# Attention on one core: the sums of K blocks for later batches on Pool instead of VectorE

## The chip, the core and the metric

The kernel runs on one core of a Trainium2 chip. The core has engines with queues of their own: TensorE (PE, matrix products), VectorE (DVE), ScalarE (ACT), Pool or GpSimd (POOL) and SyncE (SP, which here only issues transfers). Each engine runs its queue in order; between engines, semaphores order the work. The metric is device time in microseconds (us) of one launch, the median of several runs; lower is better.

## The reference

Attention without a mask, 8 batches, 2048 rows of q, k and v each, 512 columns, float32 in and out:

```python
scores = np.matmul(q, k.transpose(0, 2, 1)) / np.sqrt(d_k)
attn_weights = special.softmax(scores, axis=-1).astype(np.float32)
return np.matmul(attn_weights, v)
```

## The kernel before

**Fewer products, more sums.** Both large products are cut into 2 x 2 blocks and made with seven block products instead of eight (the Strassen-Winograd scheme). It needs sums and differences of blocks of each operand. For the scores, S^T = K Q^T, the left operand is K transposed: with its blocks a11, a12, a21, a22 four more are formed, s1 = a21 + a22, a21 = a11 - a21 (in place), s2 = s1 - a11, s4 = a12 - s2. `k_sums` (L177 to L185) makes these four for one chunk of 4 x 128 rows of K; each is one two-input instruction over 128 partitions x 512 columns in float16, all in SBUF. A batch has four chunks, `c` = 0 to 3, each with its own tiles `kraw{c}`, `ks1_{c}`, `ks2_{c}`, `ks4_{c}`; every batch overwrites those of the batch before. Likewise `q_sums` (L194) makes the sums for Q, `v_sums` (L209) those for V, and `p_sums` (L325) those for the exponentials P.

**What comes from where.** A chunk of k or q is loaded and cast to float16 by a transfer on POOL's queue (`load`, L109, into one of three `stage` buffers), and transposed by a transfer on SP's queue (`dma_transpose`, L140, into `kraw` or `qraw`). V is loaded on POOL's queue (`load_v`, L204). Results leave through SP's queue (`store`, L400).

**The main loop** (L672 to L695) runs over 32 groups `g`, four to a batch (`qt` = 0 to 3), in 28 slots each. In a slot TensorE has one of the seven products for the scores of a block that is one half batch ahead (`Group.product`, L262: 2 matmuls of 512 columns, weights from `kraw` or `ks`) and, in every second slot, one of the seven products P V (`Pair.product`, L355: 8 matmuls of 256 columns). The order of all this is written out by hand (`ORDER`, L451; `QORDER`, L456), and each engine's queue follows the program's order.

What follows a score product: a copy of x by ACT (L298), copies into `cz` by ACT (L303, L306), two additions by VectorE out of PSUM (L309 after product 7, L312 after product 3), and exponentials by ACT (L227). What follows P V: a reciprocal (L413, L419) and scaling additions (L396) on VectorE, scaled copies (L393) on ACT, and a store. The sums of P stand in slots 7 to 13 (second pair), 17 to 22 and 4 to 5 (first pair of the next group); those of Q in slots 23 to 27 of odd groups and 6 of even ones; those of V in slots 0 to 20 of a batch's first group.

**The work around the change.** `prefetch` (L483) places the next batch's loads, transposes and K sums into slots. `PLAN` (L465) says where loads and transposes stand; `KSUMS` (L480) says in which slot the four sums of a chunk are put into the queue `background`; one is taken out in each of the slots 2, 8, 10, 14, 16, 24 and 26:

```python
(0, 10, "load", "k", 0), (0, 20, "trans", "k", 0),
(0, 22, "load", "k", 1), (1, 7, "trans", "k", 1),
(1, 8, "load", "k", 2), (1, 20, "trans", "k", 2),
(1, 22, "load", "k", 3), (2, 7, "trans", "k", 3),
KSUMS = {(1, 8): 0, (1, 20): 1, (2, 6): 2, (2, 20): 3}
```

The pairs are (qt, slot). The first products that use the new chunk 0 stand in the group with qt = 2, slot 0; chunk 1's in slot 14; chunks 2 and 3 follow in qt = 3, slots 0 and 14. The first batch's own K sums are made before and in group 0, from other calls of `k_sums` (L638, L641, L533).

POOL's queue holds, in the main loop, the 84 loads for batches 1 to 7 and one small fill of a constant.

Of the kernel before, what the change touches and what calls it, by code (L numbers as in the profile page):

```python
# [12 lines left out]
def kernel(  # L13
# [21 lines left out]
    nc = tc.nc  # L35
# [73 lines left out]
    def load(what, b, c, pieces=(CH,), room=None):  # L109
        t = staged.get((what, b, c))  # L110
        if room is not None:
            t = staged[what, b, c] = room
        if t is None:
            t = staged[what, b, c] = stage.tile([P, CH, D], F16, tag="stage", name="stage")
        n = CH - sum(pieces)
        for w in pieces:
            at = c * CH + n
            nc.gpsimd.dma_start(out=t[:, n:n + w, :], in_=srcs[what][b, :, at:at + w, :])
            n += w
# [20 lines left out]
    def dma_transpose(what, b, c):  # L140
        src = staged.pop((what, b, c))
        dst = raw_of(what, b, c)
        nc.sync.dma_start_transpose(
            out=dst[:, 0:CH].rearrange("p n c r -> p (n c) r"),
            in_=src[:].rearrange("p n d -> p (n d)"),
        )
# [20 lines left out]
    def k_blocks(c):  # L167
        w = kops[c][0][:].rearrange("p (j s) c r -> p j s c r", s=2)
        return w[:, :, 0, 0:2], w[:, :, 0, 2:4], w[:, :, 1, 0:2], w[:, :, 1, 2:4]
# [4 lines left out]

    add, sub = nc.vector.tensor_add, nc.vector.tensor_sub

    def k_sums(c):  # L177
        a11, a12, a21, a22 = k_blocks(c)
        _, s1, s2, s4 = kops[c]
        return [  # L180
            lambda: add(s1[:], a21, a22),
            lambda: sub(a21, a11, a21),
            lambda: sub(s2[:], s1[:], a11),
            lambda: sub(s4[:], a12, s2[:]),
        ]  # L185
# [18 lines left out]
    def load_v(b, c):  # L204
        dst = vraw[b % 2][:].rearrange("p j s d -> p (j s) d")
        ns = slice(c * CH, (c + 1) * CH)
        nc.gpsimd.dma_start(out=dst[:, ns, 0:D], in_=srcs["v"][b, :, ns, :])
# [272 lines left out]
    KSUMS = {(1, 8): 0, (1, 20): 1, (2, 6): 2, (2, 20): 3}  # L480
    background = deque()

    def prefetch(g, slot):  # L483
        b, qt = divmod(g, NQT)
        if (g, slot) == (0, 12):
            nc.gpsimd.memset(vraw[1][:, :, 1, D:D + 1], 1.0)
        for kind, what, c in PLAN.get((qt, slot), ()):
            if b + 1 < B:
                if kind == "load":
                    load_v(b + 1, c) if what == "v" else load(what, b + 1, c)  # L490
                else:
                    dma_transpose(what, b + 1, c)
        if (qt, slot) in KSUMS and b + 1 < B:
            background.extend(k_sums(KSUMS[qt, slot]))
        if background and slot in ((2, 8, 10, 14, 16, 24, 26)):
            background.popleft()()

# [130 lines left out]
    for n, (kb, half) in enumerate([(kb, 0) for kb in range(4, 8)] + [(kb, 1) for kb in range(8)]):  # L628
        if (kb, half) == (5, 0):
            pe_transpose("k", 1, 2, 4)  # L630
        if (kb, half) == (6, 0):
            pe_transpose("q", 1)
            background.extend(q_sums(0))
        if (kb, half) == (3, 1):
            pe_transpose("k", 2)
        if (kb, half) == (6, 1):
            pe_transpose("k", 3)
            background.extend(k_sums(3))  # L638
        plain_tile(kb, half, "qz" if n % 3 == 2 else "qx")
        if (kb, half) in ((3, 1), (7, 1)):  # L640
            background.extend(k_sums(kb // CH))  # L641
        step(2)
# [29 lines left out]
    for g in range(NP):  # L672
        todo = after_slot(g)
        sp = g // 2 + 1
        more = sp < NP // 2
        for slot in range(NS + 4):
            n, at = divmod(slot, len(QORDER))
            old, what = QORDER[at]
            if slot < NS:
                if more and at == 0:  # L680
                    cur = Group(sp, g % 2 * NG + n)
                if more and old == 0:
                    cur.product(what)
                if old == 1 and prev is not None:
                    prev.product(what)
                if at == 2 and prev is not None:
                    prev.exp_right()
                if at == len(QORDER) - 1:
                    prev = cur if more else None
                for f in sums_of(g, slot):  # L690
                    f()
            if slot in todo:
                pv(g, todo[slot])
            if slot < NS:
                prefetch(g, slot)  # L695
# [30 lines left out]
```

## Time and profile before

| | |
|---|---|
| time, median of 3 runs | 804.24 us (803.97 to 804.41) |
| span of the profiled execution | 801.4 us |
| busy: PE, DVE, ACT, POOL | 794.3, 557.6, 571.7, 72.3 us |
| K sums on VectorE (L181 to L184), whole run | 128 of 0.41 us each |
| sums of 128 x 1024 columns of P on VectorE (L338 to L341) | 192 of 0.68 us each |
| additions out of PSUM on VectorE (L309, L312) | 244 of 0.69 us each |
| issue of one load on POOL | 0.74 to 0.75 us |
| issue to landing, median: load of k, of q, of v | 7.0, 8.0, 10.7 us |
| issue to landing, median: transpose of k, of q | 7.1, 6.2 us |
| granted clock of TensorE | 1.00 |

The span runs from the first to the last instruction of the profiled execution; the runs' own times, of which the table gives the median, contain a little more than that. A line of an engine's timeline reads: start, duration, engine, line of the source, operation, tiles out<-in, shape, count, and in brackets the engine's idle time before it and what ended it. A matmul's duration in such a line is longer than the distance to the next one's start, since matmuls overlap in the array. "PEld" is the loading of a matmul's weights, which runs beside the matmul before it.

### The profile page before, as it was taken

How to read it: one execution, taken by the hardware profiler on the slowest of the kernel's cores; microseconds unless marked ns; L12 is line 12 of the kernel's file. 1: busy time of each engine (PE TensorE's matmuls, PEld its weight loads, DVE VectorE, ACT ScalarE, POOL GpSimd, SP SyncE). 2: the span in 40 equal slices, each digit the busy share in tenths (PEclk: the TensorE clock that was granted, in tenths of full speed). 3: DMA queues.
4: the chain of work that ended last, by engine and by line, in shares of the span. 5: the costliest groups of instructions: out<-in, count | busy, mean ns of one | idle time of the engine just before them, and what ended most of it. 6: DMA issues, size and time to landing. Idle time of an engine off the chain costs nothing.

```text
span 801.4 us, 14572 instructions
## 1 busy us (share of the span) xinstructions
PE 794.3 (99%) x5532; PEld 535.8 (67%) x5532; DVE 557.6 (70%) x1227; ACT 571.7 (71%) x1021; POOL 72.3 (9%) x105
## 2 busy tenths in 40 slices
PE   8999999999999999999999999999999999999998
PEld 5566666666666666666666666666666666666676
DVE  4786767857577675767758677586776857668464
ACT  5677777777767767777777777777677677776752
POOL 4011110011001011011000110001100011000000
PEclk9999999999999999999999999999999999999999
DMA  9999993999929999399974999749994598711112
GB/s 223 173 173 192 195 167 78 150 192 198 156 56 166 166 157 195 78 155 194 199 125 93 164 167 191 124 93 189 168 189 113 97 219 149 156 40 40 53 44 102
DMA packets 188150, 115.80 MB, mean 144 GB/s; under 512 B 122416, under 2 KB 170800, under 8 KB 188080
## 3 DMA queue, kind: packets, MB, share of 16 engines
q0 software_dynamic: 49648, 49.29, 42.8%
q1 hardware_dynamic: 138144, 65.29, 38.0%
q8 instruction: 43, 0.70, 0.4%
q10 hardware_dynamic: 288, 0.30, 0.1%
q14 instruction: 27, 0.22, 0.1%
HBM read 100.70 MB, written 33.55 MB: 168 GB/s over the span
## 4 chain that ended last, share of the span: by engine, by line
PE 98%; DMA 1%; ACT 1%; DVE 0%; SPq 0%; issue 0%
PE t L384 49%; PE t L287 46%; PE t L234 2%; PE tr L153 1%; DMA first<-in_k_dram 1%; PE t L247 0%; ACT right L227 0%; ACT o L393 0%; SPq L128 0%; DVE cz L309 0%; ACT stage L132 0%; ACT kraw L156 0%; ACT left L227 0%; ACT cz L306 0%; DVE qraw L156 0%
## 5 line engine op out<-in xcount | busy, mean ns | idle before, releaser
L287 PE MATMUL t<-qraw,kraw 128*128 128x512 f16 x728 | 197.1, 379 | 0.2 <-ACT left L227 0.2
L393 ACT ACTIVATE o<-t,r 128x256 f32<-128x256 f32 x256 | 121.6, 475 | 99.4 <-DVE r L413 67.5
L384 PEld LDWEIGHTS <-s 128*128 128x128 f16 x1536 | 150.2, 98 | 57.0
L227 ACT ACTIVATE left<-t 128x512 f16<-128x512 f32 (+1 forms) x260 | 154.7, 597 | 38.9 <-PE t L287 33.7
L396 DVE SCALAR_TENSOR_TENSOR o<-t,r,o 128x256 f32<-128x256 f32 x192 | 92.5, 482 | 105.0 <-PE t L384 48.7
L287 PEld LDWEIGHTS <-kraw 128*128 128x128 f16 x976 | 95.4, 98 | 64.1 <-issue 0.5
L287 PE MATMUL t<-qs,ks 128*128 128x512 f16 x488 | 135.3, 379 | 0.0
L384 PE MATMUL t<-vh,left 128*128 128x256 f16 x1024 | 133.0, 273 | 0.0
L384 PE MATMUL t<-vt,s 128*128 128x257 f16 (+1 forms) x1024 | 133.0, 273 | 0.0
L227 ACT ACTIVATE right<-cz 128x1024 f16<-128x1024 f32 x122 | 129.5, 1062 | 1.8 <-DVE cz L309 1.7
L384 PEld LDWEIGHTS <-right 128*128 128x128 f16 x1024 | 100.1, 98 | 38.3 <-issue 0.4
L384 PEld LDWEIGHTS <-left 128*128 128x128 f16 x1024 | 100.2, 98 | 37.6
L303 ACT COPY cz<-t 128x512 f32<-128x512 f32 x120 | 70.4, 587 | 72.7 <-PE t L287 72.3
L309 DVE TENSOR_TENSOR cz<-t,cz 128x512 f32<-128x512 f32 x122 | 83.8, 687 | 51.7 <-PE t L287 51.6
L312 DVE TENSOR_TENSOR cz<-t,cz 128x512 f32<-128x512 f32 x122 | 84.2, 690 | 38.5 <-PE t L287 38.2
L287 PEld LDWEIGHTS <-ks 128*128 128x128 f16 x732 | 71.5, 98 | 47.9
L287 PE MATMUL t<-qraw,ks 128*128 128x512 f16 x244 | 72.6, 379 | 0.0
L287 PE MATMUL t<-qs,kraw 128*128 128x512 f16 x244 | 72.6, 379 | 0.0
L298 ACT COPY t<-t 128x512 f32<-128x512 f32 x120 | 68.4, 570 | 4.1 <-PE t L287 1.0
L306 ACT COPY cz<-t 128x512 f32<-128x512 f32 x122 | 70.9, 582 | 0.0
L384 PE MATMUL t<-vt,right 128*128 128x256 f16 x512 | 67.1, 273 | 0.0
L384 PE MATMUL t<-vh,s 128*128 128x257 f16 x512 | 66.7, 273 | 0.0
(62 smaller groups left out, 576.5 us busy)
## 6 DMA issues: line engine op xcount, KB each, us to landing
out_dram<-o SPq DMA_DIRECT2D x127, 256.0 KB, 3.5
vh<-in_v_dram POOLq DMA_DIRECT2D x32, 512.0 KB, 10.7
stage<-in_q_dram POOLq DMA_DIRECT2D x28, 512.0 KB, 8.0
stage<-in_k_dram POOLq DMA_DIRECT2D x28, 512.0 KB, 7.0
right<-in_q_dram POOLq DMA_DIRECT2D x2, 512.0 KB, 9.8
right<-in_k_dram POOLq DMA_DIRECT2D x2, 512.0 KB, 11.7
first<-in_q_dram SPq DMA_DIRECT2D x2, 256.0 KB, 3.3
cz<-in_q_dram SPq DMA_DIRECT2D x2, 256.0 KB, 5.1
```

Source lines behind the costliest of these rows:

```text
L153: nc.tensor.transpose(tr[:, m, dc, :], src[:, n + m, dc * P:(dc + 1) * P], ident[:])
L227: nc.scalar.activation(out=out_, in_=in_, func=EXP, scale=inv_sqrt_d)
L234: nc.tensor.matmul(st[:], kops[c][0][:, n, dc, :], qraw[0][:, half * NT:(half + 1) * NT, dc, :], start=(dc == 0), stop=(dc == ND - 1),)
L287: nc.tensor.matmul(dst[:], lhs[:, j, dc, :], rhs[:, :, dc, :], start=(n in (1, 5) and dc == 0), stop=(dc == 1), skip_group_check=True,)
L298: f(out=self.y[:], in_=self.x[:])
L303: f(out=self.cz[:, 1, :], in_=self.z[:])
L306: nc.scalar.copy(out=self.cz[:, 0, :], in_=self.x[:])
L309: nc.vector.tensor_add(self.cz[:, 1, :], self.x[:], self.cz[:, 1, :])
L312: nc.vector.tensor_add(self.cz[:, 0, :], self.z[:], self.cz[:, 0, :])
L384: nc.tensor.matmul(dst[:, 0:width], lhs(j), rhs(j), start=(first and j == 0), stop=(j == NJ - 1), skip_group_check=True,)
L393: nc.scalar.activation(out=out_, in_=src, func=COPY, scale=r[:])
L396: nc.vector.scalar_tensor_tensor(out=out_, in0=src, scalar=r[:], in1=out_, op0=MULT, op1=ADD)
```

## The change

`k_sums` takes the engine as an argument, VectorE if none is given. The calls from `prefetch`, which make the sums for the second and later batches (7 batches x 4 chunks x 4 sums), give Pool; the first batch's keep VectorE. The places in the program stay the same, so these instructions move from VectorE's queue into POOL's, among the loads that `prefetch` issues there.

```diff
-    def k_sums(c):
+    def k_sums(c, engine=nc.vector):
         a11, a12, a21, a22 = k_blocks(c)
         _, s1, s2, s4 = kops[c]
+        add, sub = engine.tensor_add, engine.tensor_sub
         return [
             lambda: add(s1[:], a21, a22),
...
         if (qt, slot) in KSUMS and b + 1 < B:
-            background.extend(k_sums(KSUMS[qt, slot]))
+            background.extend(k_sums(KSUMS[qt, slot], nc.gpsimd))
         if background and slot in ((2, 8, 10, 14, 16, 24, 26)):
             background.popleft()()
```

In the built program, the queues of TensorE, ScalarE and SP hold the same instructions in the same order as before. VectorE's is shorter by 112 instructions. POOL's is longer by these 112 and by one that loads a library, ahead of the first of them. In a batch POOL's queue then reads: load k2; K0 s1, a21; load v1; K0 s2, s4; load k3; K1 s1, a21; load q2; K1 s2; load q3; K1 s4; load v2; K2 s1, a21, s2; load v3; K2 s4; K3 s1, a21, s2, s4; then the next batch's load q0.

## The prediction

> **What bounds the kernel now.** I read the shares of the page first, then the stretches, then the order of time on one engine after another around one batch's sums of K blocks.
>
> ```profile
> PE 794.3 (99%) x5532; PEld 535.8 (67%) x5532; DVE 557.6 (70%) x1227; ACT 571.7 (71%) x1021; POOL 72.3 (9%) x105
> PE 98%; DMA 1%; ACT 1%; DVE 0%; SPq 0%; issue 0%
> ```
>
> The second line is the chain that ended last: TensorE alone. The share of a busy PE is modelled, so I checked it against the spacing of starts, in the order of time on TensorE and in the table of stretches (span of the stretch, then busy time of PE, PEld, DVE, ACT, POOL):
>
> ```profile
> 180.38 1.04 PE L384 MATMUL t<-vh,s 128*128 128x257 f16 x8
> 181.26 0.59 PE L287 MATMUL t<-qs,ks 128*128 128x512 f16 x2
> 181.69 0.59 PE L287 MATMUL t<-qs,kraw 128*128 128x512 f16 x2
> 183.86 1.04 PE L384 MATMUL t<-vt,s 128*128 128x256 f16 x8
> 159.90:184.20 24.30, 24.30 (x171) 16.41 (x169) 15.84 (x34) 17.94 (x33) 5.09 (x7) 1.00 1.10 178
> 184.20:208.60 24.40, 24.40 (x171) 16.52 (x169) 17.68 (x40) 18.00 (x33) 1.48 (x2) 1.00 1.19 198
> ```
>
> A matmul of 512 columns starts every 0.215 us (0.59 less its own 0.38), one of 257 every 0.11 us, and no time is left over in the stretches, at a granted clock of 1.00. Idle of TensorE is 801.4 - 794.3 = 7.1 us, nearly all before the first batch's steady work and after the last scores. So VectorE, at 70%, has nothing to sell: unloading it can't shorten the chain. The change can only keep the time or lengthen it. A batch repeats every 97.46 us; I work with the one whose sums are wanted around 163 to 225 us.
>
> **The change, part by part.** *Removed from VectorE:* 7 batches x 4 chunks x 4 = 112 sums, 0.414 us each (the groups of L181 to L184, 0.412 to 0.416): 46.4 us, 6.6 us a batch. Worth nothing, since no matmul of the steady part waits for VectorE except one of 0.10 us a batch (154.7 us, waiting for the sums of V); 7 x 0.1 = 0.7 us is the most that relief could return, and that wait is over before the K sums begin. I count 0.
>
> *Added to POOL:* the same 112 sums, and one instruction that loads a library ahead of the first. POOL's queue holds its loads too, in program order: load k2, two sums of chunk 0, load v1, two sums, load k3, two of chunk 1, load q2, a sum, load q3, a sum, load v2, three of chunk 2, load v3, one, then chunk 3's four. POOL isn't tied to VectorE's place in the program, so a sum runs as soon as its transposed chunk has landed.
>
> *Is a sum late for TensorE?* Landings of chunks 0 to 3, from the tile view of kraw: 162.6, 177.5 (issued 168.52, the longest landing, 9.0), 181.0, 198.4. The first weight loads that want the sums come at 186.4, 198.5, 210.7 and 222.9, the last sum of a chunk some 2 us after. Between landing and need lie 23.8, 21.0, 29.7 and 24.5 us. Tightest is the whole run of chunks 1 to 3: twelve sums and four loads of 0.74 us between 177.5 and 224.9, (47.4 - 3.0) / 12 = 3.7 us a sum. Only a sum longer than that would be late. Nothing.
>
> *Loads behind the sums.* Load k3 starts at 163.19 now and goes behind four sums and load v1, 6 us later; it takes 7.0 us to land and its transpose is issued at 192.96: 16 us to spare. Load q2 (178.71) moves to about 181, wanted at 196.49, 8 us to land: 7 us to spare. v1 to v3 feed sums of the next batch, 40 us on. SP's queue keeps its order. Cost 0; without that cover each us of lateness would be one on TensorE.
>
> *The library.* No row shows it. Below: 0. Above: in the first batch chunk 0 lands at 70.7 and is wanted at 186.4 - 97.5 = 88.9, and POOL is free from 61.2 (load k2 at 60.44), so with four sums and a load still to come some 20 us is hidden. I take 0.
>
> *What a sum takes on POOL.* No two-input row on POOL exists. Lower end: 0.42 us, VectorE's. Upper end: POOL's memsets of 8 and 1 columns took 0.133 and 0.099 us, 4.9 ns a column; 512 of these and the 0.19 us of a one-column copy make 2.7 us. The geometric middle is 1.06; if POOL doesn't pair 16-bit elements, the lower end is VectorE's 32-bit 0.69 and the middle 1.36. I take 1.2.
>
> *What it does to VectorE.* This is where I expect the cost, and one pair of rows points at it:
>
> ```profile
> 38.79 0.69 DVE L198 TENSOR_TENSOR qs<-qraw 128x1024 f16<-128x1024 f16 x1 [1.01 <-DMA qraw<-right]
> 39.40 0.75 DVE L216 TENSOR_TENSOR vt<-vh,vt 128x512 f16<-128x512 f16 x2
> 38.83 0.70 POOL L620 CAST gate<-qraw 128x1 f32<-128x1 f16 x1 [22.97 <-DMA qraw<-right]
> 39.59 0.27 POOL L621 CAST gate<-vh 128x1 f32<-128x1 f16 x1
> ```
>
> A cast of one column on POOL took 0.70 us, and ended 0.05 us after the VectorE sum that had started before it; its twin ended 0.05 us after the first of the next two (39.40 + 0.41). The one without such company, L564, took 0.19. So POOL's read was held by a VectorE instruction with two SBUF inputs. The other direction no row shows: its bounds are no hold at all and a hold for a POOL sum's whole length. I take the whole length, since both casts were held to the very end. Instructions with one input in PSUM (L309, L312, L396) I take as free: L312 started beside POOL's load at 40.11 without growing.
>
> The Trainium skill says that it does: SBUF — State Buffer, section "Who interferes with whom", has an exclusive lock between a VectorE instruction with two SBUF inputs and a GpSimd one that reads SBUF; whoever starts first keeps it. No run here shows the direction that matters. By it the sum is the one below, without it zero. The GPSIMD Engine Reference, section "Performance versus the Vector engine", has 4497 ns for a two-input add of 2048 columns; a quarter is an estimate of 1.12 us, by which the walk below ends near 0.2 us a batch, at 805.6.
>
> **The walk** (VectorE's K sums taken out, 1.2 us a sum, 0.1 between dependent ones). VectorE and ScalarE now:
>
> ```profile
> 177.97 0.55 DVE L339 TENSOR_TENSOR s<-s,left 128x768 f16<-128x768 f16 x1
> 180.15 0.69 DVE L309 TENSOR_TENSOR cz<-t,cz 128x512 f32<-128x512 f32 x1 [1.09 <-PE t L287]
> 181.82 0.16 DVE L419 RECIPROCAL r<-t 128x1 f32<-128x1 f32 x1
> 182.23 0.68 DVE L199 TENSOR_TENSOR qs<-qraw,qs 128x1024 f16<-128x1024 f16 x1
> 188.81 0.28 DVE L338 TENSOR_TENSOR s<-right 128x256 f16<-128x256 f16 x1
> 182.02 0.47 ACT L393 ACTIVATE o<-t,r 128x256 f32<-128x256 f32 x1
> 182.86 0.61 ACT L227 ACTIVATE left<-t 128x512 f16<-128x512 f32 x1
> ```
>
> Chunk 0 (from 162.65): its four sums hold L338 or L339 by at most 1.2 us, with 0.9 to 1.4 us of idle time behind each. Chunk 1, first sum 177.55 to 178.75: L339 is held 0.78. Second sum 179.3 to 180.5: L340 is held, and behind it L309, wanted at 180.15, starts at 181.0, 0.85 late; the matmul that reuses its bank starts at 181.69, 0.85 after L309's end of 180.84: just covered. Load q2, third sum 181.24 to 182.44: L341 is held. Load q3, fourth sum 183.6 to 184.8. The reciprocal L419 comes 1.68 late, and with it ACT's L393, which ended at 182.49 and whose bank PE takes at 183.86: 1.37 of cover, so TensorE waits 0.28. ACT's L227 behind it (ended 183.47, bank taken at 184.73, 1.26) is 1.65 late: 0.39 in all. L199 is held to 184.8. Chunk 2 follows: its first sum holds L200, its third, 188.72 to 189.92, holds L338, which ends 1.1 late; the weight load that wants it comes 0.53 after its end, 0.92 with the wait already had: 0.2 more. Chunk 3 (198.4 on) meets sums with 1.5 to 2.5 us behind them: 0. A batch: 0.28 + 0.11 + 0.2 = 0.6 us; 7 batches 4.2 us.
>
> The profiled span is 801.4; the median of the runs lies 2.8 us above, which I take as outside the span and unchanged. 804.24 + 4.2 = **808.4 us**.
>
> **Rivals.** *No change:* VectorE isn't held, or a POOL sum is under about 1.1 us and every lateness stays inside 0.85, 1.37, 1.26 and 0.53. For: those covers; TensorE waits for nothing now. Against: the two casts. Time 804.2, at best 803.5 with the 0.7 us back. This is the side on which it isn't slower; the point is 0.85 us of lateness at L309.
>
> *A longer sum on POOL:* at 1.6 us the six waits before L338 grow by 0.4 each, 2.4 us, with the cover already spent: 3.0 a batch, 21 in all, 825 us. For: the memset slope (2.7 would give 9.6 a batch, 871). Against: a slope from eight columns is rough.
>
> *Late loads or sums:* needs 7 us of delay at q2 or 20 us of library. Each us beyond costs one: some 810, against it the spare times above.
>
> **How the numbers follow.** Forecast (805.9 to 815) 0.46; no change 0.30; longer sums (815 and up) 0.20; late loads 0.02; faster 0.02. About 0.2% (1.6 us) is what a measurement of this kernel tells from no change. Slower: 0.46 + 0.20 + 0.02 = 0.68; within 0.30; faster 0.02. The range holds the no-change case and most of the longer sums: 803.7 to 822; the forecast's own is 805.9 to 815.
>
> **What would show it.** After: 112 POOL sums of about 1.2 us in bursts after each landing; VectorE's two-input sums stretched beyond 0.68 only where such a burst runs, L309 and L312 not; gaps of 0.1 to 0.3 us on TensorE in the 15 us after chunk 1 has landed, none elsewhere. It is wrong if L339 keeps 0.68 us beside a POOL sum, if gaps come at the weight loads of ks, or if TensorE waits in stretches without POOL work.

## The result: 13 us slower, and the profile after

| | before | changed |
|---|---|---|
| time, median | 804.23 us | 817.11 us (813.21 to 820.93) |
| span of the profiled execution | 801.4 us | 819.1 us |
| ratio to before | | 1.0154, 95% interval 1.0130 to 1.0177 |

The forecast was 808.4 us: the direction and the mechanism came as forecast, the loss was 12.9 us instead of 4.2. The profiled execution of the changed kernel is the longest of its four (820.93 us). In the changed kernel every line from 178 on stands one further down: the first sum of Q, L198 before, is L199 now.

The busy shares and the chain that ended last, of the changed kernel:

```profile
PE 800.2 (98%) x5532; PEld 536.0 (65%) x5532; DVE 576.1 (70%) x1115; ACT 569.3 (70%) x1021; POOL 214.0 (26%) x217
PE 80%; DMA 8%; DVE 4%; POOL 3%; issue 2%; ACT 2%; SPq 0%; ACTq 0%; DVEq 0%; POOLq 0%
```

VectorE lost 112 instructions and is busy for 18.5 us longer than before. Its remaining two-input sums are longer than before by 56 us in all, counted by their lengths: an instruction that is held counts as busy. The chain, TensorE alone before, now runs through VectorE and POOL too, and through landings of transfers (8%, most of them those that release POOL's sums and those at the start). Groups of instructions (count, busy us, mean ns, idle time before):

```profile
L199 DVE TENSOR_TENSOR qs<-qraw 128x1024 f16<-128x1024 f16 x16 | 20.6, 1285 | 3.3 <-DMA qraw<-right 2.5 <-ACT qraw L156 0.8
L182 POOL TENSOR_TENSOR ks<-kraw 128x512 f16<-128x512 f16 x28 | 35.0, 1251 | 142.7 <-DMA kraw<-stage 104.3 <-PE t L288 19.3 <-PE t L385 19.0
```

The first sum of Q takes 1.29 us in the mean instead of 0.69, with two inputs in SBUF; L310 and L313, with one input in PSUM, kept 0.68 and 0.69. What TensorE waited for, in the view of waits (us in total, times, longest):

```profile
PE t L385 <- ACT o L394: 7.7, 9, 2.2
PE t L288 <- DVE cz L310: 1.7, 3, 1.3
PE t L288 <- POOL ks L182: 0.9, 3, 0.3
```

The largest place is the scaled copy behind a late reciprocal, the first place of the walk. The third row isn't a late K sum: the matmuls wait there on VectorE's semaphore, and chunk 2's first sum, which happened to end last, isn't wanted for more than 20 us.

One burst in order of time. POOL first, from the load behind chunk 1's second sum on (L184 and L185 are chunk 1's third and fourth sums, the last L182 is chunk 2's first), then VectorE, ACT and TensorE:

```profile
383.14 0.79 POOL L118 DMA_DIRECT2D stage<-in_q_dram  x1
383.94 1.17 POOL L184 TENSOR_TENSOR ks<-ks,kraw 128x512 f16<-128x512 f16 x1
385.05 0.79 POOL L118 DMA_DIRECT2D stage<-in_q_dram  x1
385.85 1.16 POOL L185 TENSOR_TENSOR ks<-kraw,ks 128x512 f16<-128x512 f16 x1
386.95 0.79 POOL L208 DMA_DIRECT2D vh<-in_v_dram  x1
387.76 1.54 POOL L182 TENSOR_TENSOR ks<-kraw 128x512 f16<-128x512 f16 x1
...
384.13 1.41 DVE L342 TENSOR_TENSOR s<-left,s 128x768 f16<-128x768 f16 x1
385.45 2.83 DVE L199 TENSOR_TENSOR qs<-qraw 128x1024 f16<-128x1024 f16 x1
388.21 0.15 DVE L420 RECIPROCAL r<-t 128x1 f32<-128x1 f32 x1
...
388.40 0.47 ACT L394 ACTIVATE o<-t,r 128x256 f32<-128x256 f32 x1 [2.73 <-DVE r L420]
...
386.16 0.59 PE L288 MATMUL t<-qraw,kraw 128*128 128x512 f16 x2
388.93 0.92 PE L385 MATMUL t<-vt,s 128*128 128x256 f16 x7 [2.18 <-ACT o L394]
```

L199 begins at 385.45, while POOL only issues a load; the next sum is recorded 0.40 us later. With the port free it would have been done at 386.14. It takes 2.83 us, of which 0.69 are its own: it is held through that sum, which ends at 387.01, and some 0.6 us more, through most of the load after it. The reciprocal, the scaled copy and TensorE follow, one behind the other, and TensorE stands for 2.18 us.

### The profile page after: what moved, and what is told of

The parts are those of the page before. It is cut to its first block, busy times and chain, and to the rows that moved or that the text cites. A ratio compares the mean times of both kernels' runs of the same rounds, so it can differ in the third digit from the quotient of the medians.

```text
span 819.1 us, 14631 instructions
## 1 busy us (share of the span) xinstructions
PE 800.2 (98%) x5532; PEld 536.0 (65%) x5532; DVE 576.1 (70%) x1115; ACT 569.3 (70%) x1021; POOL 214.0 (26%) x217
## 4 chain that ended last, share of the span: by engine, by line
PE 80%; DMA 8%; DVE 4%; POOL 3%; issue 2%; ACT 2%; SPq 0%; ACTq 0%; DVEq 0%; POOLq 0%
PE t L385 42%; PE t L288 38%; DMA kraw<-stage 3%; DMA qraw<-right 2%; DMA right<-in_q_dram 2%; POOL ks L182 1%; DMA out_dram<-o 1%; DVE qs L199 1%; DVE cz L310 1%; DVE right L341 1%; DMA first<-in_k_dram 1%; POOL stage L118 1%; ACT right L228 0%; ACT left L228 0%; ACT o L394 0%
## 5 line engine op out<-in xcount | busy, mean ns | idle before, releaser
L313 DVE TENSOR_TENSOR cz<-t,cz 128x512 f32<-128x512 f32 x122 | 83.9, 687 | 45.1 <-PE t L288 39.9
L310 DVE TENSOR_TENSOR cz<-t,cz 128x512 f32<-128x512 f32 x122 | 83.5, 684 | 36.4 <-PE t L288 36.1
L208 POOL DMA_DIRECT2D vh<-in_v_dram x32 | 24.8, 775 | 182.0 <-PE t L385 179.5
L182 POOL TENSOR_TENSOR ks<-kraw 128x512 f16<-128x512 f16 x28 | 35.0, 1251 | 142.7 <-DMA kraw<-stage 104.3
```

Source lines behind the costliest of these rows:

```text
L310: nc.vector.tensor_add(self.cz[:, 1, :], self.x[:], self.cz[:, 1, :])
L313: nc.vector.tensor_add(self.cz[:, 0, :], self.z[:], self.cz[:, 0, :])
```

## The experiments

Each changes the kernel before or the changed one. Ratios are to the kernel before, run on the same chip among them (804.2 to 804.5 us).

### Is taking the sums off VectorE worth anything?

```diff
-        dst = raw_of(what, b, c)
+        dst = raw_of(what, b, c) if what == "q" or b == 0 else unused
...
-            background.extend(k_sums(KSUMS[qt, slot]))
+            background.extend([lambda: None] * 4)
```

> Leaves out the K sums of the second and later batches on both engines; those batches go on with the first batch's K. It shows what taking the sums off VectorE is worth by itself. All theories: TensorE has no slack to give, so 804.2 us, at best 803.5; POOL as before, VectorE's sums of Q at 0.68 us.

Measured 804.80 us, ratio 1.0012 (0.9987 to 1.0036). Unloading VectorE by 46 us is worth nothing, as the stretches of the profile had it.

### POOL sums that nothing waits for

```diff
+    def side_sums(c):
+        a12 = k_blocks(c)[1]
+        return [lambda: nc.gpsimd.tensor_add(side[:], a12, a12)] * 4
...
-            background.extend(k_sums(KSUMS[qt, slot]))
+            background.extend(
+                (lambda f=f, s=s: (f(), s()))
+                for f, s in zip(k_sums(KSUMS[qt, slot]), side_sums(KSUMS[qt, slot]))
+            )
```

> VectorE makes all K sums as before, and POOL makes 112 further sums of the same size at the same places, which nothing reads. Theory HOLD (a POOL sum keeps VectorE's sums with two SBUF inputs waiting, and VectorE's lateness reaches TensorE): slower than before by at least the 13 us of the change, 815 to 835 us, with VectorE's sums of Q (L198, L199 before) stretched well over 0.68 us. Rival LATE SUMS (TensorE waits for sums that POOL finishes late): 804.2 us, as nothing waits for these. Rival LATE LOADS (the sums stand before loads in POOL's queue): about 817 us with VectorE's sums unstretched.

Measured 822.01 us, ratio 1.0213 (1.0175 to 1.0251). TensorE's sums are VectorE's here and no matmul waits for one in the trace, and the loss is there and larger. LATE SUMS falls.

### POOL instructions that read nothing

The same with fills. Each chunk's first fill follows a one-column copy from the landed chunk; 512 columns in the first run, 1280 in the second.

```diff
+        fill = lambda: nc.gpsimd.memset(side[:], 1.0)
+
+        def first():
+            nc.gpsimd.tensor_copy(out=tick[:], in_=a12[:, 0, 0, 0:1])
+            fill()
+
+        return [first, fill, fill, fill]
```

> As the run with further sums on POOL, but each is a fill of a tile of the same size, which reads nothing from SBUF; one column of the landed chunk is read ahead of each chunk's first fill, so that it starts at the same time. HOLD, in the form that only reading instructions hold: 804.2 to 805 us, VectorE's sums at 0.68. LATE LOADS: slower in proportion to the fills' length, 817 us if a fill takes 1.2 us. If fills hold VectorE as well, 815 us and stretched sums.

> As the run with fills on POOL, which took 0.53 us each; now 1280 columns, so that a fill takes about as long as a sum, 1.15 to 1.35 us. HOLD by reading instructions: 804.2 to 805 us, VectorE's sums at 0.68. LATE LOADS: about 817 us.

Measured 804.59 us, ratio 0.9997 (0.9983 to 1.0010), with fills of 0.53 us, and 804.75 us, 1.0012 (0.9993 to 1.0031), with fills of 1.18 us, as long as a sum, in the same places among the loads. No sum of VectorE is longer than before. The long fills, two groups of POOL and VectorE:

```profile
L182 POOL MEMSET side<- 128x1280 f16 x112 | 131.6, 1175 | 3.2
L211 DVE TENSOR_TENSOR qs<-qraw 128x1024 f16<-128x1024 f16 x16 | 11.0, 685 | 2.6 <-DMA qraw<-right 1.8 <-ACT qraw L156 0.8
```

So neither POOL's being busy nor what stands before its loads makes the loss. The sums make it, and what they do and the fills don't is read SBUF. LATE LOADS falls for the changed kernel.

### Which chunks

```diff
-            background.extend(k_sums(KSUMS[qt, slot], nc.gpsimd))
+            on = nc.gpsimd if KSUMS[qt, slot] in (0, 3) else nc.vector
+            background.extend(k_sums(KSUMS[qt, slot], on))
```

> Only the sums of chunks 0 and 3 move to POOL; those of chunks 1 and 2 stay on VectorE. HOLD: the stalls of the changed kernel all lie in the 20 us after chunk 1 has landed, so most of the loss goes: 804.2 to 807 us, with single stretched sums after chunks 0 and 3. LATE SUMS or LATE LOADS: half of the sums, about half of the loss, 810 us.

> The other half: only the sums of chunks 1 and 2 move to POOL; those of chunks 0 and 3 stay on VectorE. HOLD: the whole loss, 813 to 820 us. LATE SUMS or LATE LOADS: half of it, 810 us.

> Only chunk 1's sums move to POOL, the other chunks' stay on VectorE. HOLD with the waits of TensorE set in chunk 1's burst: most of the loss, 809 to 815 us. If the loss comes from the long run of chunks 1 and 2 together: 804.2 to 807 us.

> The kernel with chunks 0 and 3 on POOL once more, with more rounds: 803.3 to 804.4 us, no change that this measurement can tell; HOLD has no place at which it could be faster, TensorE having no time to give.

| chunks on POOL | median | ratio (95% interval) |
|---|---|---|
| 0 and 3 | 803.91 us | 0.9989 (0.9979 to 0.9998) |
| 0 and 3, again | 803.60 us | 0.9994 (0.9983 to 1.0004) |
| 1 and 2 | 815.15 us | 1.0138 (1.0117 to 1.0159) |
| 1 | 808.91 us | 1.0058 (1.0040 to 1.0076) |

Half of the sums cost nothing, as the walk had it; the other half carries some 11 of the 13 us, and chunk 1 alone some 4.7, just under what was expected. VectorE is held after chunks 0 and 3 too (26 sums of VectorE, 17 us in all in the trace), but idle time follows there. The small gain of the first run isn't told from no change by the second.

### Loads between the sums

The walk let VectorE have the port while POOL issued a load between two sums. The burst above says otherwise, so the loads were moved, in the list of places. No load between any sums (all four sums of a chunk issued at once, at slots (1, 16), (2, 8) and (2, 26)):

```diff
-    KSUMS = {(1, 8): 0, (1, 20): 1, (2, 6): 2, (2, 20): 3}
+    KSUMS = {(1, 16): (0,), (2, 8): (1, 2), (2, 26): (3,)}
```

> All sums on POOL as in the changed kernel, but no load stands between them in POOL's queue: chunk 0's four behind load v1, chunks 1 and 2's eight behind load q3, chunk 3's four behind load v3. Theory THROUGH LOADS (a sum behind a load takes the port while the load is still being issued, so that VectorE is held through two sums and a load, up to 2.15 us): here no two-input sum of VectorE takes more than 1.9 us (0.68 and one POOL sum of 1.2), most of the loss goes, 804.5 to 809 us. Rival PLAIN LENGTH (single holds of 1.2 us add up to the loss): holds and loss as in the changed kernel, 811 to 820 us.

Measured 815.81 us, ratio 1.0138 (1.0120 to 1.0156). The holds shrank as THROUGH LOADS says: 36 us in all instead of 56, and only two of 52 over 1.25 us (1.37; both began during load q3, which stands directly ahead of the eight sums). The time didn't: the burst of eight now starts 4 to 11 us later (counted by TensorE's matmuls, chunk 1's first sum of each batch), on top of the short sums of P in slots 4 and 5 and of L310. Its moving spoiled this run as a test.

Two loads put between chunk 3's sums, where no loss was:

```diff
-        (2, 10, "load", "v", 2), (2, 20, "load", "v", 3),
+        (3, 2, "load", "v", 2), (3, 8, "load", "v", 3),
```

> As the run with chunks 0 and 3 on POOL (803.9 us, longest sum of VectorE 1.6 us), but loads v2 and v3 stand between chunk 3's sums in POOL's queue. THROUGH LOADS: among VectorE's sums after chunk 3's landing some are held longer than one POOL sum, over 1.9 us in all; the time rises if that meets a short cover, 804 to 808 us. PLAIN LENGTH: no sum of VectorE over 1.9 us, 803.9 us.

Measured 810.41 us, ratio 1.0082 (1.0053 to 1.0111): 6 us from two loads' places. Of VectorE's sums after chunk 3's landing only one went over 1.9 us (2.84; another, of 1.93, began during load v1, between chunk 0's sums), so the time came out beyond what was expected and the lengths short of it; chunk 3's burst also began some 3 us earlier here, so this run too moved more than one thing.

Load q3 behind chunk 1's last sum, all chunks on POOL; then v2 and v3 behind chunk 2's last as well:

```diff
-        (2, 0, "load", "q", 2), (2, 6, "load", "q", 3),
+        (2, 0, "load", "q", 2), (2, 9, "load", "q", 3),
...
-        (2, 10, "load", "v", 2), (2, 20, "load", "v", 3),
+        (2, 25, "load", "v", 2), (2, 25, "load", "v", 3),
```

> The changed kernel with one load moved by one place in POOL's queue: load q3 stands behind chunk 1's fourth sum instead of ahead of it. THROUGH LOADS: VectorE's first sum of Q (L199), 2.1 to 2.8 us in most batches of the changed kernel, stays at or under 1.9 us; TensorE's wait for the scaled copy behind it (0.5 to 2.3 us a batch) falls below 1.4 us or goes; 807 to 813 us. PLAIN LENGTH: L199 and the time as in the changed kernel, 813 to 821 us.

> As the run with load q3 behind chunk 1's sums, and loads v2 and v3 behind all of chunk 2's, so that only load q2 is left between sums of chunks 1 and 2. THROUGH LOADS: no sum of VectorE over 1.9 us there. Time: 806 to 812 us if the waits were set by the longest holds; 813 us and more if a longer unbroken run of sums over VectorE's late sums of P costs as much, as in the run without loads between.

Measured 814.26 us, 1.0130 (1.0097 to 1.0163), and 809.36 us, 1.0064 (1.0048 to 1.0079). In the first, TensorE's waits before the matmuls that follow the scaled copy fell from 6.8 us in all to 2.0, but those at the next place grew; its time missed the band by 1.3 us. L199 still reaches 2.1 us where it begins during load q2, which was left in place: "at or under 1.9" was stated too tightly. In the second more than half of the loss is gone with all 112 sums on POOL; four sums of VectorE pass 1.9 us there, all four begun during a load that still has a sum behind it.

The clean test moves nothing but this one load, with chunk 1 alone on POOL (the last run of the table above is its counterpart):

> Only chunk 1's sums on POOL (808.9 us), with load q3 behind its fourth sum instead of ahead of it; nothing else differs, and no burst of chunk 2 follows. THROUGH LOADS: VectorE has the port between the third and fourth sum, so TensorE's wait for the scaled copy (0.8 to 1.7 us a batch there) mostly goes: 804.2 to 806.5 us. PLAIN LENGTH: 808 to 810 us.

Measured 806.38 us, ratio 1.0022 (1.0007 to 1.0038), against 808.91 us. The burst of the same batch, q3 ahead of the fourth sum (POOL, then VectorE):

```profile
379.34 1.17 POOL L184 TENSOR_TENSOR ks<-ks,kraw 128x512 f16<-128x512 f16 x1
380.46 0.79 POOL L118 DMA_DIRECT2D stage<-in_q_dram  x1
381.26 1.17 POOL L185 TENSOR_TENSOR ks<-kraw,ks 128x512 f16<-128x512 f16 x1
...
380.86 2.13 DVE L199 TENSOR_TENSOR qs<-qraw 128x1024 f16<-128x1024 f16 x1
```

and q3 behind it:

```profile
378.26 1.17 POOL L184 TENSOR_TENSOR ks<-ks,kraw 128x512 f16<-128x512 f16 x1
379.51 1.36 POOL L185 TENSOR_TENSOR ks<-kraw,ks 128x512 f16<-128x512 f16 x1
380.81 0.79 POOL L118 DMA_DIRECT2D stage<-in_q_dram  x1
...
379.78 1.64 DVE L199 TENSOR_TENSOR qs<-qraw 128x1024 f16<-128x1024 f16 x1
```

L199 is held 0.95 us instead of 1.44; from the chunk's first sum (376.02 and 374.93) it ends after 6.5 us instead of 7.0. TensorE's waits for the scaled copy behind chunk 1's bursts fall from 3.5 us in three batches to 2.0 in four. The first trace has one more such wait, of 1.7 us at 321.0, but no POOL sum is near it. The scaled copy waited there for the landing of a store that empties its output buffer:

```profile
320.48 0.47 ACT L394 ACTIVATE o<-t,r 128x256 f32<-128x256 f32 x1 [2.88 <-DMA out_dram<-o]
```

So the medians put some 2.5 of the 4.7 us on one load's place, the waits in the two traces some 1.5. How often a late store adds to the time wasn't counted over runs.

The same over eleven traces (all runs with POOL sums that aren't paced; a sum counts if it began over 0.08 us before the load's recorded end): 82 two-input sums of VectorE began while POOL issued a load with a sum directly behind it. 66 were held: 58 until that sum's end (0.12 to 0.13 us before its recorded end), 8 longer, to within 0.4 us of the end of one more load that had a sum behind it. Of the 16 that weren't, 14 began in the first 0.13 us of the issue. 221 began during a load with no sum directly behind it: none was held. (One more, begun in the last 0.08 us of a load that had a second load and then a sum behind it, was held.) So it isn't the load that holds VectorE but the sum behind it, before its recorded start.

### One sum at a time

All sums on POOL, each behind a one-column copy that waits for the newest exponential at its place in the program; then the same with loads k3, q2 and q3 moved to (1, 12), (1, 23) and (2, 0).

```diff
     def exp(out_, in_):
         nc.scalar.activation(out=out_, in_=in_, func=EXP, scale=inv_sqrt_d)
+        newest[0] = out_
...
+            at = newest[0]
+            at = at[:, 0, 0:1] if len(at.shape) == 3 else at[:, 0:1]
+            nc.gpsimd.tensor_copy(out=pace[:], in_=at)
             background.popleft()()
```

> The changed kernel, but each POOL sum first waits, by a one-column copy on POOL, for the newest exponential at its place in the program, so that sums come singly, two or more slots (1.7 us) apart, as they did on VectorE. HOLD with covers of 0.5 to 1.7 us: single holds of at most 1.2 us, mostly covered, 804.2 to 807 us. If single holds cost as much as bursts: 813 us and more.

> The paced kernel, whose times spread from 804.0 to 813.7 us, with its loads k3, q2 and q3 moved ahead of sums that made them late (k3 behind chunk 0's second sum, q2 ahead of chunk 1's first, q3 behind its second). If the spread is LATE LOADS, made by the pacing: 804.0 to 806 us in all runs, with all 112 sums on POOL. If single holds cost it: 807 us and more.

Measured 810.25 us (804.02 to 813.66), ratio 1.0068 (1.0041 to 1.0094), against what was expected; its profiled run, of 803.0 us span, shows no hold over 0.84 us and no lost time in six of seven batches. In the seventh TensorE waited 1.26 us, and not for a hold: the scaled copy waited for a store that landed 11.1 us after its issue (the median before is 3.5), within 0.3 us of a transpose of q and of load v3.

```profile
120.62 0.47 ACT L397 ACTIVATE o<-t,r 128x256 f32<-128x256 f32 x1 [3.84 <-DMA out_dram<-o]
```

With the three loads moved: 804.56 us, ratio 1.0008 (0.9994 to 1.0022), one run of twelve over 806 (809.35; of the kernel before, two of 29). So the places of the loads made the spread, and with them moved 112 sums on POOL cost nothing that can be measured. That pacing had made transfers late, the rival that falls for the changed kernel, fits both runs, but no paced run over 806 us was profiled: how the time was lost in those is not shown. The six paced runs of 810 us and more have granted clocks of 0.994 to 0.998, the other four 1.00, so TensorE at lower speed is a part of it. In the trace with the loads moved VectorE is still held 28 times, 15 us in all, never over 0.94 us. None of the kernels is told to be faster than the one before.

## Why the prediction failed

- *TensorE has no time to give, relief is worth nothing:* right (the run without sums).
- *Sums and loads in time on POOL:* right for the changed kernel (sums that nothing waits for; fills). The library showed no cost: the first POOL sum starts when its chunk has landed and takes 1.15 us.
- *A sum on POOL takes 1.2 us:* 1.15 us where POOL isn't held itself, 1.25 to 1.30 in the mean with its own holds. The rival of longer sums falls. A quarter of the figure in the Trainium skill's GPSIMD Engine Reference, section "Performance versus the Vector engine", an estimate of 1.12 us, agrees with the rows.
- *The hold goes both ways, and only two SBUF inputs are held:* right. The section "Who interferes with whom" of the skill's SBUF — State Buffer says the same, down to fills that only write: no sum of VectorE stretched beside them.
- *Chunks 0 and 3 cost nothing, the gaps come after chunk 1:* right, but for single waits of TensorE at the start that differ between runs.
- *The step that failed* is in the walk: "Load q3, fourth sum 183.6 to 184.8. The reciprocal L419 comes 1.68 late". It gave VectorE's first sum of Q the port while load q3 was issued. With a sum of 1.15 us and the port taken through the load, the same rows read: third sum to 182.3, load to 183.1, fourth sum to 184.25, the sum of Q only then, to 184.8, and the reciprocal 2.9 us late. Less the 1.37 of cover that is 1.55 us of TensorE's time instead of 0.28, 1.3 us more a batch, 9 in all: 817 us. This was worked out afterwards, and that it meets the median is partly luck: that wait measured 0.55 to 2.3 us in five batches and nothing in two, 6.8 in all against the walk's 2.0. Matmul by matmul against the kernel before, TensorE falls 16.2 us behind in the profiled execution from 50 us on: the 6.8 at this wait, 1.8 at a lower clock behind one of them (see the last section), and some 7.7 at other places, all behind chunk 1's landing, for which the walk had 0.11 and 0.2 us a batch, 2.2 in all. So the walk's other terms were too small as well, by more than three times. Each batch's landings fall differently on VectorE's order, which is likely also why the runs spread over 8 us where those of before, in the same comparison, spread over 0.4.

What moving the one load showed is a part: 2.5 of chunk 1's 4.7 us by the medians, 1.5 by the waits in the traces. What is left there are mostly holds of about one sum's length, more than the walk had. How the loss of chunks 1 and 2 divides between long holds and the places that a longer burst reaches was not separated.

## What to carry to other kernels

An engine with nothing to give to the critical path isn't worth unloading, and an idle engine isn't free to use: what it shares with a busy one comes first. Before VectorE's two-input sums are put beside POOL's, look how much cover stands behind each, add up whole bursts rather than single holds, and keep POOL's sums single and without a load directly ahead of them. If a queue's order allows the work anywhere in a long stretch, the place decides: here the same 112 sums cost 13 us or nothing.

## What the runs showed of the hardware that was not expected

*A POOL sum behind a load takes the port early*, as counted above: 66 of 82 against 0 of 221. The GPSIMD Engine Reference of the skill, section "Architecture", has POOL as eight cores of which each starts the next instruction once its own share is done, and section "When to use GPSIMD" has a pair of them make a load's descriptors. That would let the other six begin the sum during the load. No run here shows single cores, so this cause is argued, not shown.

*Half speed after a short wait.* Behind the wait of 2.18 us above TensorE ran slowly for some 3.4 us. The table of stretches (span, busy PE, PEld, DVE, ACT, POOL, then the granted clock):

```profile
386.00:389.60 3.60, 1.42 (x11) 0.84 (x10) 3.57 (x3) 1.20 (x3) 3.50 (x4) 1.00 1.16 214
389.60:393.40 3.80, 3.80 (x17) 2.08 (x15) 2.90 (x6) 1.67 (x4) 3.78 (x4) 0.55 1.19 193
```

A clock of 0.55 over 3.8 us is 1.7 us lost on top of the wait; from 390 to 392 us it was 0.50. A wait nearly as long in the next batch (start to start 2.28 us more than usual, against 2.34) had no such sequel. In the run with chunks 1 and 2 on POOL a wait of 1.99 us had it again (0.50 from 90 to 92 us). The skill's TensorE: Matmul & The Clock Gate, section "What's actually happening", has the array throttled after an idle window of about 3.4 us; here a wait well under that was enough twice.

*Fills on POOL* took 0.53 us for 512 columns and 1.18 for 1280, 0.84 ns a column; the slope of 4.9 ns that the prediction took from two tiny fills for its upper end was nearly six times too steep.
